# Spreading modulation sums, splitting weight sums from their copies, and other places for the last down weights, in a two-layer hybrid block

## The chip, the cores and the metric

One NeuronCore of a Trainium2 chip runs the whole program. The metric is the device time of one execution in microseconds (us), the median over the runs; lower is better. The engines are TensorE (PE, matmuls; PEld its weight loads), VectorE (DVE), ScalarE (ACT), GpSimd (POOL) and SyncE (SP). Each works through its own instructions in order. In this kernel SP and POOL do little but issue DMAs.

## The reference

A sequence of 512 tokens with 1024 features passes through two layers of three sub-blocks each. A sub-block i modulates its input, applies a function, and normalizes the gated sum:

```
mod = (silu(c) @ ada_w[layer] + ada_b[layer]).reshape(B, 3, 3, D_MODEL)
...
shift, scale, gate = mod[:, 0, None], mod[:, 1, None], mod[:, 2, None]
y = fn(x * (1 + scale) + shift)
return layer_norm(DEEPNORM_ALPHA * x + res_w * (1 + gate) * y, ln_g, ln_b)
```

The functions are, in order: SwiGLU with 2816 hidden features, `(silu(h @ w_gate) * (h @ w_up)) @ w_down`; in the first layer a mixer of a chunked mLSTM and a dilated attention, in the second one of a short convolution and a gated spatial unit; SwiGLU again. All inputs are float32.

## The kernel before

**Phases.** The program runs six phases, i = 0 to 5, one for each sub-block: feed-forward (0, 2, 3, 5), mixer 0 (1) and mixer 1 (4). Activations lie with features on partitions: X holds x, and XH and XL a high and a low part (float32r) of the modulated input. Every product of two float32 operands is made of three matmuls (`mm3`, L468 to L472): high by high, high by low, low by high. So every weight tile must be split as well: ACT copies the raw tile to its high part, DVE subtracts to get the low part (L302 and L305).

**Weights.** `plan` (L200) lists all weight tiles ("units") in their order of use. `load` (L258) issues the next raw tile's DMA on SP, with two raw buffers. `halve` (L277) takes one step of splitting the oldest raw tile: half of it, two steps to a unit. A unit's split parts go to a class of places: "w" (three places, kept through all phases) or "d" (two places of a feed-forward phase). A unit may be split when the unit so many before it in its class is done with (`ready`, L267).

**Feed-forward.** The 22 hidden tiles are worked in three chunks c of 6, 8 and 8: up (gate and up products, SiLU, product), then down, added to X by `resid` (L641), one instruction to an output tile. In chunks 1 and 2 the up part uses a Strassen-like scheme (`seven`, L766): two 4-tile halves of the contraction, two halves of the tokens, seven products instead of eight for gate and up together. It needs sums of the moving operand (`sums_of`, L740, made during the down part of chunk 0, kept in the two "d" places until the last product of chunk 2) and sums of the weights, `sr` (made in `quarter`, L313). There a unit is split in four steps, u.n = 0 to 3, and each step's parts go to one of three "w" places, used in a ring (`Ring`, L169):

- step 0: DVE makes sums 0 and 1 (L326, L327); ACT copies the raw upper tile;
- step 1: DVE makes sums 2 and 3 (L329, L330); ACT copies sums 0 and 1 (L338);
- step 2: ACT copies sums 2 and 3; step 3: ACT copies the last raw quarter.

Each step's low half (L341) is issued one piece later. `quarters` (L350) makes up for steps that are late when a product needs them.

**Order of work.** The order on every engine is written out by the program. `run` (L455) issues a list of pieces, each some 12 matmuls of 256 columns or 6 of 512, and calls `tick` (L443) after each. A tick may load; then it does one modulation sum if the count of ticks is a multiple of `ticks["ada"]`, else a step of splitting (on odd ticks, or on all where the list is "eager"), else a deferred ACT instruction. Lists called "quiet" have no ticks; there `prepare` (a load and a step) is placed by hand (SPLIT_A, SPLIT_B, SPLIT_MIX).

**Modulation.** mod is not a matmul here. For each phase there are 24 tiles of 128x1024 of ada_w: 8 of shift, 8 of scale, 8 of gate. `ada_load` (L384) brings one on POOL's queue into one of two buffers; `ada_sum` (L390) multiplies it with silu(c) and sums along the row, one DVE instruction (L392). `ada_step` does the next sum in a queue of all phases' tiles. Phase 0's first 16 are made in `start` (L1520), which interleaves them with the first weights and rows of x. Its 8 gate tiles and all of phases 1 to 5 come by ticks. ADA_EVERY (L48) gives the ticks between two sums, for the first up part of a phase, the down parts and the mixers. `ada_finish(i + 1)` in the last projection, between its first half of the tokens and its second, makes all sums of phase i + 1 that are still missing, and phase 0's missing gates are made after its first up part (L912).

**The last projection** (`last_projection`, L690) of a phase does the down products of chunk 2 for the first half of the tokens, then for the second half, with the first half's layer norm placed between the second's pieces (NORM_A): centre (L554), squares (L556, L564), statistics (L580, L512 to L526), spread (L586). The second half's norm goes between the first pieces of the next phase (NORM_B).

Of the kernel before, what the change touches and what calls it, by code (L numbers as in the profile page):

```python
# [19 lines left out]
P = 128  # L20
# [24 lines left out]
NORM_V_AT = (1, 5)  # L45


ADA_EVERY = {"up": (3, 0, 0, 0, 0, 0), "down": ((0, 2, 2), 0, (0, 2, 0), (0, 2, 0), 0, (0, 0, 0)), "mixer": (0, 4, 0, 0, 4, 0)}  # L48


C_C = 0
# [20 lines left out]
def tile_kernel(ctx, tc, prm, crow, cst, mst, oneh, relb, xin, adaw, wgu, wd6, wd8, abfm, abtm, abg, about, cdfm, cdtm, cdout,  # L72
# [127 lines left out]
    def plan():  # L200
        def add(src, shape, cls="w", i=0):
            u = Unit(src, shape, cls, i)
            units.append(u)
            members.setdefault((cls, i if cls != "w" else 0), []).append(u)

        def add_seven(src, i, ring, t):

            u = Unit(src, [2, KT, P], "s", i)
            u.ring, u.t, u.parts = ring, t, []
            units.append(u)  # L210

        def hold(i):

            held_d[i] = [Unit(None, None, "d", i) for _ in range(2)]
            members.setdefault(("d", i), []).extend(held_d[i])

        for i in range(6):
            if i in FFN_OF:
                f = FFN_OF[i]
                j0 = 0  # L220
                for c, n in enumerate(CHUNKS):
                    for j in range(j0, j0 + n):
                        if c:
                            if j == j0:
                                ring = Ring(n, i)
                                members["w", 0].extend(ring.places)
                            add_seven(wgu[f, j], i, ring, j - j0)
                        else:
                            add(wgu[f, j], [2, KT, P], "d" if j in ((3, 4) if i else (4,)) else "w", i)
                    if c == 0:  # L230
                        hold(i)
                    for g in range(4):
                        add(wd6[f, g] if n == 6 else wd8[f, c - 1, g], [2, n, P], "d" if c == 2 and g > 2 else "w", i)
                    j0 += n
            elif i == 1:
                for u in range(2):
                    add(abtm[0, u], [4, S])
                add(abfm[0], [2, KT, P])
                add(abg, [1, KT, P], "g", i)
                add(abfm[1], [2, KT, P], "k", i)  # L240
                for n in (2, 4, 3, 5):
                    add(abfm[n], [2, KT, P])
                for u in range(2):
                    add(abtm[1, u], [4, S])
                for n in (6, 7):
                    add(abfm[n], [2, KT, P])
                for c in range(2):
                    for g in range(2):
                        add(about[c, g], [4, 4, P])
            else:  # L250
                for u in range(2):
                    add(cdtm[u], [4, S])
                for n in (0, 1, 2, 3, 6, 4, 5, 7):
                    add(cdfm[n], [2, KT, P], "e" if n == 1 else "w", i)
                for g in range(4):
                    add(cdout[g], [2, KT, P], "w" if g < 3 else "e", i)
# [56 lines left out]
    def quarter(u):  # L313

        at = u.ring.part(u)
        if u.i not in sums_at or not at:
            return False
        place = u.ring.places[at[0]]
        if place.hl is None:
            if not ready(place):  # L320
                return False
            place.hl = tuple(wp.tile([P, 2, KT, P], F32R, tag="w" + x, name=nm("w" + x)) for x in "hl")
        sr = sums_at[u.i]
        a11, a12, a21, a22 = (u.raw[:, m, 4 * k:4 * k + 4, :] for m in range(2) for k in range(2))
        if u.n == 0:
            V.tensor_tensor(out=sr[:, 0], in0=a21, in1=a22, op=ALU.add)  # L326
            V.tensor_tensor(out=sr[:, 1], in0=sr[:, 0], in1=a11, op=ALU.subtract)  # L327
        elif u.n == 1:
            V.tensor_tensor(out=sr[:, 2], in0=a11, in1=a21, op=ALU.subtract)  # L329
            V.tensor_tensor(out=sr[:, 3], in0=a12, in1=sr[:, 1], op=ALU.subtract)  # L330
        src = (u.raw[:, 0], sr[:, 0:2].rearrange("p a b c -> p (a b) c"), sr[:, 2:4].rearrange("p a b c -> p (a b) c"),
               u.raw[:, 1, 4:8, :])[u.n]
        k0 = 4 * (u.t % 2) if u.n == 3 else 0
        h, l = (t[:, at[1], k0:k0 + src.shape[1], :] for t in place.hl)
        u.parts.append((h, l))
        u.n += 1
        last = u.n == 4
        A.copy(h, src)  # L338

        def low():  # L340
            V.tensor_tensor(out=l, in0=src, in1=h.bitcast(F32), op=ALU.subtract)  # L341
            u.lows += 1
            if last:
                u.split = True
                halved[0] += 1
        begun[0] += last
        after(1, low)
        return True
# [35 lines left out]
    def ada_load(i, t):  # L384
        l, s3 = divmod(i, 3)
        w = ap_.tile([P, D], F32, tag="aw", name=nm("aw"))
        nc.gpsimd.dma_start(w, adaw[l, s3 * 24 + t])  # L387
        return w

    def ada_sum(i, t, w):  # L390
# [11 lines left out]
    def ada_step():  # L402
        if not (ada_l or ada_q):
            return False
        ada_ahead()
        ada_sum(*ada_l.pop(0))
        return True
# [3 lines left out]
    def ada_scalars(i):  # L411

        g = prm_t[:, C_LNG + (i - 1) * 8:C_LNG + i * 8]
        b = prm_t[:, C_LNB + (i - 1) * 8:C_LNB + i * 8]
        At = SM([P, 8], tag="At", bufs=2)
        Bt = SM([P, 8], tag="Bt", bufs=2)
        V.scalar_tensor_tensor(out=At, in0=mod[i][:, 8:16], scalar=1.0, in1=g, op0=ALU.add, op1=ALU.mult)
        V.scalar_tensor_tensor(out=Bt, in0=mod[i][:, 8:16], scalar=1.0, in1=b, op0=ALU.add, op1=ALU.mult)
        V.tensor_tensor(out=Bt, in0=Bt, in1=mod[i][:, 0:8], op=ALU.add)
        scal["A", i], scal["B", i] = At, Bt  # L420
        ag = SM([P, 8], tag="ag", bufs=2)
        ab = SM([P, 8], tag="ab", bufs=2)
        V.tensor_scalar(out=ag, in0=g, scalar1=ALPHA, scalar2=None, op0=ALU.mult)
        V.tensor_scalar(out=ab, in0=b, scalar1=ALPHA, scalar2=None, op0=ALU.mult)
        scal["ag", i], scal["ab", i] = ag, ab

    def ada_gate(i):
        Gt = SM([P, 8], tag="Gt", bufs=2)
        V.tensor_scalar(out=Gt, in0=mod[i][:, 16:24], scalar1=1.0, scalar2=RW[i], op0=ALU.add, op1=ALU.mult)
        scal["G", i] = Gt  # L430

    def ada_finish(i):
        while ada_l and ada_l[0][0] <= i or not ada_l and ada_q and ada_q[0][0] <= i:
            ada_step()
        if i < 6:
            ada_scalars(i)
            ada_gate(i)


    defer = []  # L440
# [199 lines left out]

    def resid(i, d, ps, cs):  # L641

        V.scalar_tensor_tensor(out=X[:, d, cs], in0=ps, scalar=scal["G", i][:, d:d + 1], in1=X[:, d, cs],  # L643
                               op0=ALU.mult, op1=ALU.add)

# [87 lines left out]
    def ffn(i, f, hp):  # L733
# [119 lines left out]
        for c, n in enumerate(CHUNKS):  # L853
# [54 lines left out]
                free(u)  # L908
                jj += 1
            flush(defer)  # L910
            ticks["ada"] = ADA_EVERY["down"][i][c]
            if i == 0 and c == 0:  # L912
                while ada_l and ada_l[0][0] == 0 or ada_q and ada_q[0][0] == 0:
                    ada_step()
                ada_gate(0)

            def operands(u, d, k, cs):
                h, l = u.hl
# [6 lines left out]
                moving_sums = [f for k in range(4) for f in sums_of(k)]  # L925
            if c < len(CHUNKS) - 1:
                for g in range(4):
                    u = take()
                    ps = []
                    for d in (2 * g, 2 * g + 1):  # L930
                        if c == 0:
                            for f in moving_sums[3 * d // 2:3 * (d + 1) // 2]:
                                ps.append(lambda f=f, d=d: after(1 + (d % 2), f))
                        ps.append(pieces(lambda k, u=u, d=d: operands(u, d, k, FULL), n, S, lambda ps, d=d: resid(i, d, ps, FULL)))
                    if rest_:
                        a, b = ps
                        run([rest_[0]] + a[:2] + [rest_[1]] + b[:2] + a[2:] + b[2:], eager=True)
                        rest_ = []
                    else:
                        for p in ps:  # L940
                            if callable(p):
                                p()
                            else:
                                run(p, eager=g == 3)
                    free(u)
            else:
                us = units[used[0]:used[0] + 4]
                used[0] += 4
                last_projection(i, us, lambda d, k, cs: operands(us[d // 2], d, k, cs), n,
                                (rest_[0], lambda: (rest_[1](), free(*held_d[i]))))  # L950
# [785 lines left out]
```

## Time and profile before

| | |
|---|---|
| time, median of 3 runs | 2000.06 us (1997.52 to 2003.45) |
| the profiled execution: time | 2002.09 us |
| its span, first to last instruction | 2000.3 us |
| PE busy | 1890.6 us, 95%, 12954 matmuls |
| DVE busy | 1457.9 us, 73% |
| ACT busy | 836.9 us, 42% |
| POOL busy | 68.4 us, 3% |
| mean granted clock of PE | 0.978 |
| read from HBM | 255.41 MB |

How to read it: busy time is the time in which the engine's row of the trace shows an instruction. Matmuls are pipelined and their ends are modelled, so what tells is PE's idle time and the rate at which matmuls start. In a row of waits, "PE pa L777 <- DVE wl L341" says that a matmul of line 777 into tile pa stood still until the DVE instruction of line 341 that writes wl was through. In a row of a group of instructions, the last column is the engine's idle time before them and what ended most of it. In a row of the timeline come start, duration, engine, line, operation, out<-in, and in brackets the idle time before it. In a table of windows come the stretch (us from the start of the span), its width, each engine's busy time with the number of its instructions, the granted clock, the share of the DMA engines in use, and GB/s. PE was idle for 109.7 us of the span, in waits of up to 14 us.

### The profile page before, as it was taken

How to read it: one execution, taken by the hardware profiler on the slowest of the kernel's cores; microseconds unless marked ns; L12 is line 12 of the kernel's file. 1: busy time of each engine (PE TensorE's matmuls, PEld its weight loads, DVE VectorE, ACT ScalarE, POOL GpSimd, SP SyncE). 2: the span in 40 equal slices, each digit the busy share in tenths (PEclk: the TensorE clock that was granted, in tenths of full speed). 3: DMA queues.
4: the chain of work that ended last, by engine and by line, in shares of the span. 5: the costliest groups of instructions: out<-in, count | busy, mean ns of one | idle time of the engine just before them, and what ended most of it. 6: DMA issues, size and time to landing. Idle time of an engine off the chain costs nothing.

```text
span 2000.3 us, 31495 instructions
## 1 busy us (share of the span) xinstructions
PE 1890.6 (95%) x12954; PEld 1732.3 (87%) x12954; DVE 1457.9 (73%) x2694; ACT 836.9 (42%) x1398; POOL 68.4 (3%) x133
## 2 busy tenths in 40 slices
PE   6999989999999999998998999899699899999997
PEld 5889889888777998987998899799698799898997
DVE  6698787856566838868775588796699783884875
ACT  4445155253343544524525255153342253452541
POOL 0000100000000000010000000100001000000000
PEclk9999999999999999998999999999799999999998
DMA  9533644434453322254322224633425421232321
GB/s 344 171 106 112 211 146 142 149 131 145 136 183 93 111 70 85 105 201 148 127 96 81 89 85 142 213 120 127 137 95 211 178 93 69 84 116 85 106 106 43
DMA packets 57381, 259.56 MB, mean 130 GB/s; under 512 B 6083, under 2 KB 15724, under 8 KB 38549
## 3 DMA queue, kind: packets, MB, share of 16 engines
q1 hardware_dynamic: 38804, 190.44, 26.9%
q0 software_dynamic: 18432, 67.12, 9.9%
q8 instruction: 101, 1.65, 0.3%
q14 instruction: 44, 0.35, 0.1%
HBM read 255.41 MB, written 2.12 MB: 129 GB/s over the span
## 4 chain that ended last, share of the span: by engine, by line
issue 63%; PE 26%; DVE 4%; POOL 2%; DMA 2%; ACT 1%; SPq 0%; POOLq 0%; DVEq 0%; ACTq 0%
PE pm L470 6%; PE pm L472 6%; PE pm L471 6%; PE pm L777 4%; PE pa L777 3%; POOL aw L387 2%; DMA aw<-in_adaw 2%; DVE aw L392 1%; DVE wl L341 0%; PE pb L580 0%; ACT wh L338 0%; PE pa L543 0%; ACT w L556 0%; PE pa L1134 0%; PE pa L471 0%
## 5 line engine op out<-in xcount | busy, mean ns | idle before, releaser
L470 PE MATMUL pm<-hH,wh 128*128 128x512 f32 (+1 forms) x768 | 271.0, 353 | 11.0 <-DVE X L643 11.0
L471 PE MATMUL pm<-hL,wh 128*128 128x512 f32 (+1 forms) x768 | 269.6, 351 | 0.0
L472 PE MATMUL pm<-hH,wl 128*128 128x512 f32 (+1 forms) x768 | 269.2, 351 | 0.0
L392 DVE CUSTOM_DVE_ANT_0 aw<-aw,sc_t,prm_t 128x1024 f32<-128x1024 f32 x144 | 183.6, 1280 | 84.7 <-DMA aw<-in_adaw 84.5
L777 PE MATMUL pm<-th,wh 128*128 128x256 f32 x1024 | 239.9, 283 | 0.0
L777 PE MATMUL pa<-XH,wl 128*128 128x256 f32 x768 | 217.0, 283 | 18.5 <-DVE wl L341 18.5
L305 DVE TENSOR_TENSOR wl<-raw,wh 128x1024 fp32r<-128x1024 f32 (+1 forms) x168 | 194.8, 1169 | 51.1 <-ACT wh L302 50.8
L777 PE MATMUL pa<-XH,wh 128*128 128x256 f32 x768 | 216.2, 282 | 14.9 <-ACT pa L811 13.2
L470 PE MATMUL pm<-XH,wh 128*128 128x256 f32 (+1 forms) x632 | 214.0, 339 | 15.0 <-ACT wh L1553 14.0
L777 PE MATMUL pm<-th,wl 128*128 128x256 f32 x768 | 217.3, 283 | 0.0
L777 PE MATMUL pa<-XL,wh 128*128 128x256 f32 x768 | 215.3, 280 | 0.4 <-DVE XL L763 0.4
L471 PE MATMUL pm<-XL,wh 128*128 128x256 f32 (+1 forms) x632 | 209.6, 332 | 1.1 <-DVE XL L1601 1.1
L472 PE MATMUL pm<-XH,wl 128*128 128x256 f32 (+1 forms) x632 | 209.5, 331 | 0.0
L302 ACT CAST wh<-raw 128x1024 fp32r<-128x1024 f32 (+1 forms) x168 | 164.1, 1002 | 51.3 <-PE pm L471 26.5
L777 PEld LDWEIGHTS pm<-th,wh 128*128 128x128 f32 x1024 | 177.8, 191 | 0.4
L470 PEld LDWEIGHTS pm<-hH,wh 128*128 128x128 f32 x768 | 146.9, 191 | 31.6 <-DVE X L643 11.2
L341 DVE TENSOR_TENSOR wl<-sr,wh 128x1024 fp32r<-128x1024 f32 x128 | 156.3, 1221 | 15.9 <-ACT wh L338 14.5
L338 ACT CAST wh<-sr 128x1024 fp32r<-128x1024 f32 x128 | 134.0, 1047 | 80.7 <-DVE sr L327 49.3
L472 PEld LDWEIGHTS pm<-hH,wl 128*128 128x128 f32 x768 | 146.5, 191 | 20.5
L471 PEld LDWEIGHTS pm<-hL,wh 128*128 128x128 f32 x768 | 146.8, 191 | 20.0
L777 PEld LDWEIGHTS pa<-XH,wl 128*128 128x128 f32 x768 | 146.6, 191 | 19.6 <-DVE wl L341 19.5
L643 DVE SCALAR_TENSOR_TENSOR X<-pm,sm,X 128x256 f32<-128x256 f32 (+1 forms) x168 | 97.4, 582 | 87.8 <-PE pm L472 87.8
(295 smaller groups left out, 4557.8 us busy)
## 6 DMA issues: line engine op xcount, KB each, us to landing
raw<-in_wgu SPq DMA_DIRECT2D x84, 1024.0 KB, 4.8
aw<-in_adaw POOLq DMA_DIRECT2D x128, 512.0 KB, 3.9
raw<-in_wd SPq DMA_DIRECT2D x32, 1024.0 KB, 4.8
raw<-in_wd SPq DMA_DIRECT2D x16, 768.0 KB, 4.3
aw<-in_adaw SPq DMA_DIRECT2D x16, 512.0 KB, 8.6
raw<-in_abfm SPq DMA_DIRECT2D x8, 1024.0 KB, 4.8
raw<-in_cdfm SPq DMA_DIRECT2D x8, 1024.0 KB, 6.2
raw<-in_wgu SPq DMA_DIRECT2D x16, 256.0 KB, 8.6
```

What stands on the lines that cost most here:

```text
L302: A.copy(u.hl[0][:, x], u.raw[:, x])
L305: V.tensor_tensor(out=u.hl[1][:, x], in0=u.raw[:, x], in1=u.hl[0][:, x].bitcast(F32), op=ALU.subtract)
L338: A.copy(h, src)
L341: V.tensor_tensor(out=l, in0=src, in1=h.bitcast(F32), op=ALU.subtract)
L387: nc.gpsimd.dma_start(w, adaw[l, s3 * 24 + t])
L392: V.tensor_tensor_reduce(out=w, in0=w, in1=sc_t, scale=1.0, scalar=prm_t[:, c0:c0 + 1], op0=ALU.mult, op1=ALU.add, accum_out=mod[i][:, t:t ...
L470: T.matmul(ps, st[0], mv[0], start=first, stop=False)
L471: T.matmul(ps, st[0], mv[1], start=False, stop=False)
L472: T.matmul(ps, st[1], mv[0], start=False, stop=last)
L643: V.scalar_tensor_tensor(out=X[:, d, cs], in0=ps, scalar=scal["G", i][:, d:d + 1], in1=X[:, d, cs], op0=ALU.mult, op1=ALU.add)
L777: T.matmul(ps_, s_, v_, start=first and k + x == 0, stop=k == 3 and x == 2, skip_group_check=not first)
```

## The change

- The counts of ADA_EVERY change. A down part's count no longer depends on the phase: none in chunks 0 and 2, every third tick in chunk 1. The first up parts of phases 2, 3 and 5 get sums too (every third tick); that of phase 0 every second tick, the mixers every third. Phase 0's last down part keeps every second tick.
- In the last quarter (g == 3) of a down part of chunks 0 and 1 no sums are made.
- `ada_finish` makes only the first 16 tiles (shift and scale) of the next phase. The gates may come later, at the latest before the first `resid` of their phase. The list of phase 0's missing gates after its first up part goes.
- Phase 0's tiles that come by ticks (the 8 gates) are loaded on SP's queue, in the program's order, not on POOL's.
- In `quarter` sums 2 and 3 are a step of their own, between steps 0 and 1; a unit takes five steps.
- Of the four groups of down weights of chunk 2 the last two are of class "d", not the last alone, so they take the places that held the moving sums.

```diff
-ADA_EVERY = {"up": (3, 0, 0, 0, 0, 0), "down": ((0, 2, 2), 0, (0, 2, 0), (0, 2, 0), 0, (0, 0, 0)), "mixer": (0, 4, 0, 0, 4, 0)}
+ADA_EVERY = {"up": (2, 0, 3, 3, 0, 3), "down": (0, 3, 0), "mixer": (0, 3, 0, 0, 3, 0)}
...
-                        add(wd6[f, g] if n == 6 else wd8[f, c - 1, g], [2, n, P], "d" if c == 2 and g > 2 else "w", i)
+                        add(wd6[f, g] if n == 6 else wd8[f, c - 1, g], [2, n, P], "d" if c == 2 and g > 1 else "w", i)
...
-        elif u.n == 1:
+        elif not u.summed:
             V.tensor_tensor(out=sr[:, 2], in0=a11, in1=a21, op=ALU.subtract)
             V.tensor_tensor(out=sr[:, 3], in0=a12, in1=sr[:, 1], op=ALU.subtract)
+            u.summed = True
+            return True
...
-        nc.gpsimd.dma_start(w, adaw[l, s3 * 24 + t])
+        (nc.gpsimd if i else nc.sync).dma_start(w, adaw[l, s3 * 24 + t])
...
+    def ada_until(i, n):
+        while (ada_l or ada_q) and (ada_l or ada_q)[0][:2] < (i, n):
+            ada_step()
+
     def ada_finish(i):
-        while ada_l and ada_l[0][0] <= i or not ada_l and ada_q and ada_q[0][0] <= i:
-            ada_step()
         if i < 6:
+            ada_until(i, 16)
             ada_scalars(i)
-            ada_gate(i)
...
     def resid(i, d, ps, cs):
 
+        if ("G", i) not in scal:
+            ada_until(i, 24)
+            ada_gate(i)
...
-            ticks["ada"] = ADA_EVERY["down"][i][c]
-            if i == 0 and c == 0:
-                while ada_l and ada_l[0][0] == 0 or ada_q and ada_q[0][0] == 0:
-                    ada_step()
-                ada_gate(0)
+            ticks["ada"] = 2 if i == 0 and c == 2 else ADA_EVERY["down"][c]
...
             if c < len(CHUNKS) - 1:
                 for g in range(4):
+                    if g == 3:
+                        ticks["ada"] = 0
```

More of the change, by code (lines that the diff above doesn't have):

```diff
@@ L208, in add_seven @@
             u = Unit(src, [2, KT, P], "s", i)
-            u.ring, u.t, u.parts = ring, t, []
+            u.ring, u.t, u.parts, u.summed = ring, t, [], False
             units.append(u)
```

## The prediction

> **What bounds the kernel now.** I read the page first, then what TensorE (PE) waited for, then stretches of the span around each wait, then the order of the work inside three of them. All times are those of the profiled execution: 2002.09 us, of which 2000.3 are its span; the median of the runs is 2000.06, so I subtract from the one and give the answer on the other.
>
> ```profile
> span 2000.3 us, 31495 instructions
> PE 1890.6 (95%) x12954; PEld 1732.3 (87%) x12954; DVE 1457.9 (73%) x2694; ACT 836.9 (42%) x1398; POOL 68.4 (3%) x133
> L392 DVE CUSTOM_DVE_ANT_0 aw<-aw,sc_t,prm_t 128x1024 f32<-128x1024 f32 x144 | 183.6, 1280 | 84.7 <-DMA aw<-in_adaw 84.5
> ```
>
> PE is the bound: 95% busy, 110 us idle. No matmul is removed, so the change can only win idle time, and time in which the matmuls run slowly. The third row is the suspect: 144 modulation sums of 1.28 us on VectorE (DVE), before which DVE sat 84.5 us waiting for their tiles. DVE works in order, so whatever is queued behind such a sum waits too. Who among PE's work paid for it?
>
> ```profile
> PE pa L777 <- DVE wl L341: 18.5, 5, 6.2
> PE pb L580 <- DVE w L564: 14.9, 5, 7.9
> PE pm L470 <- ACT wh L1553: 14.0, 1, 14.0
> PE pa L777 <- ACT pa L811: 13.2, 8, 1.8
> PE pm L470 <- DVE X L643: 13.0, 4, 11.0
> PE pa L543 <- DVE w L651: 4.3, 1, 4.3
> PE pm L471 <- DVE wl L305: 3.1, 1, 3.1
> PE pm L470 <- ACT dh L302: 2.9, 2, 1.9
> PE pm L472 <- DVE dl L305: 2.3, 3, 0.8
> ```
>
> (Columns: us in total, times, longest.) Waits of 3 to 14 us carry most of it, nearly all on DVE: low halves of weights (L341, L305), norm and residual (L564, L643, L651). Their places, one row for each:
>
> ```profile
> core 0: us, PE busy (x) PEld busy (x) DVE busy (x) ACT busy (x) POOL busy (x), PEclk, DMA share, GB/s
> 118.00:126.00 8.00, 4.89 (x32) 4.07 (x31) 7.62 (x15) 2.27 (x5) 0.00 (x0) 1.00 0.00 1
> 255.00:268.00 13.00, 7.83 (x46) 7.33 (x45) 11.50 (x16) 5.06 (x9) 1.05 (x2) 0.74 0.57 205
> 902.00:920.00 18.00, 10.98 (x79) 10.28 (x77) 15.43 (x25) 5.21 (x10) 2.65 (x5) 0.81 0.66 220
> 1015.00:1034.00 19.00, 15.13 (x111) 14.82 (x110) 14.11 (x41) 3.35 (x5) 1.59 (x3) 0.91 0.26 84
> 1060.00:1082.00 22.00, 16.76 (x122) 15.74 (x121) 15.14 (x28) 11.66 (x21) 0.00 (x0) 0.92 0.34 123
> 1290.00:1302.00 12.00, 5.38 (x31) 4.98 (x31) 10.06 (x15) 3.50 (x6) 1.06 (x2) 0.72 0.59 203
> 1395.00:1428.00 33.00, 20.23 (x142) 19.63 (x141) 21.30 (x52) 4.30 (x6) 3.72 (x7) 0.79 0.34 112
> 1440.00:1453.00 13.00, 9.88 (x35) 7.73 (x35) 9.22 (x17) 6.76 (x9) 0.00 (x0) 0.74 0.62 208
> 1585.00:1609.00 24.00, 16.09 (x104) 15.65 (x103) 16.79 (x45) 4.65 (x7) 1.06 (x2) 0.79 0.21 65
> 1850.00:1863.00 13.00, 12.46 (x99) 11.89 (x98) 8.53 (x12) 6.71 (x12) 0.00 (x0) 1.00 0.22 81
> ```
>
> Width less PE's busy time is its idle time. The last row is the control: the third chunk of the last feed-forward layer (phase 5) starts with no sums before it and idles 0.5 us; the three like starts behind a down projection full of sums (255, 902, 1290) idle 5.2, 7.0 and 6.6. Eight rows also show a granted clock (PEclk) well under 1.
>
> **The sums, counted.** A tick follows each piece of matmul work (12 matmuls of 256 columns or 6 of 512, 1.4 us); ADA_EVERY says how many ticks lie between two sums. Counting ticks (16 in phase 0's first chunk, 34 in a middle down projection, of which the last 8 now take none, 18 in a last projection, 106 in mixer 0, 28 in a later first chunk, 80 in mixer 1), I get for the new kernel: phase 0 does its 8 gate sums in the 16 ticks, then 9 and 9; mixer 0 does 36 where it did 26; phases 2 and 3 do 9 and 10 in their first chunks and 9 and 8 in the middle; mixer 1 does 27 where it did 20; phase 5 the last 3. At the end of each phase the next one needs only its first 16 tiles: it has 18, 24, 24, 18 and 21. So no burst is left in ada_finish, where the old count left 3, 7 and 4 sums (1015, 1395, 1585), nor after the first chunk (3).
>
> *Bursts at a phase's end.* Idle 3.9, 12.8 and 7.9 us. What is late next is the norm's own chain, centre, squares, statistics, which these rows put behind the sums; I leave 2 us in all. Gain 22.6 (bounds 15 to 24).
>
> *Starts of the third chunk.* 17.5 us gained against the control (18.8 less three times 0.5), since the last quarter of the down projection now splits weights on every tick and the sums before it come every third tick (4.2 us) instead of every second, at which DVE waited for tiles (84.5 us in all). Bounds 10 to 17.5.
>
> *Phase 0, first chunk.* The 3.1 us at 118 follow from the burst of three that held the moving sums back; 2.6 gained (0 to 3.1).
>
> *Start.* PE begins at 14.0, with DMA saturated. Two tiles that are not needed for 50 us go first on POOL's queue:
>
> ```profile
> 1.26 1.19 POOL L387 DMA_DIRECT2D aw<-in_adaw  x2 [0.81 <-POOLq L1724]
> 0.00:20.00 20.00, 6.03 (x14) 4.64 (x15) 9.28 (x18) 7.03 (x10) 1.39 (x6) 1.00 0.92 327
> aw<-in_adaw POOLq DMA_DIRECT2D x128, 512.0 KB, 3.9
> ```
>
> On SP they queue behind the start's loads: 1 MB at 327 GB/s is 3.2 us less in the way. I take 2 (0 to 3.2). In exchange SP now waits for a sum before each of the six later tiles, with the raw weight loads for the first down projection behind it, and those feed the split on ACT and DVE; a sum every second tick is 2.8 us against 3.9 to land, two in flight: cost 1 (0 to 3).
>
> *The place.* The third group of last down weights waited for ring place 2, and that place is left with the last product, exactly when the moving sums' places are; so the group itself is no earlier or later. But place 2 is then free for the next phase's first unit, which formerly waited for a group to finish its second half. Its two steps (copy and low half) move into the first half's idle ticks, and every later step of SPLIT_A reaches one unit further. That takes away most of the weight waits at 1060 (5.2 us: dh 2.9, dl 2.3) and 1440 (3.1): gain 7.8 (4 to 8.3).
>
> *Slow tails.* After each of these idles the granted clock is halved for a while:
>
> ```profile
> 261.00:266.00 5.00, 4.53 (x21) 4.24 (x21) 4.96 (x8) 3.07 (x6) 0.00 (x0) 0.50 0.80 285
> 934.00:938.00 4.00, 4.00 (x22) 4.00 (x23) 3.98 (x6) 2.75 (x4) 0.00 (x0) 0.62 0.67 250
> 1603.00:1607.00 4.00, 4.00 (x21) 4.00 (x21) 3.28 (x14) 0.00 (x0) 0.00 (x0) 0.50 0.00 0
> 1880.00:1900.00 20.00, 20.00 (x174) 20.00 (x173) 18.45 (x29) 11.60 (x20) 0.00 (x0) 1.00 0.30 106
> ```
>
> At full clock 174 matmuls take 20 us, 0.115 each; 21 took 4 us at 1603, so 1.6 us was lost there, and about 2 at 261. Eight idles that I remove or shorten have such a tail: 8 x 1.6 = 12.8 us (6 to 16). [...]
>
> *Sums one step ahead.* A unit of the seven products now takes five steps, not four; same instructions. In that stretch DVE is 18.45 of 20 us busy, so their order matters. Here is the second unit's first sum copy, and what bounds it:
>
> ```profile
> 1851.99 1.38 PE pm L777 x12
> ```
>
> ```profile
> 1858.51 1.05 ACT L338 CAST wh<-sr 128x1024 fp32r<-128x1024 f32 x1 [0.30 <-DVE sr L327]
> 1861.07 1.22 DVE L341 TENSOR_TENSOR wl<-sr,wh 128x1024 fp32r<-128x1024 f32 x1
> 1861.18 0.42 ACT L822 ACTIVATE w<-w 128x256 f32<-128x256 f32 x1 [1.62 <-DVE w L821]
> 1875.04 0.36 ACT L811 COPY pa<-pm 128x256 f32<-128x256 f32 x1
> 1884.42 0.37 ACT L811 COPY pa<-pm 128x256 f32<-128x256 f32 x1
> ```
>
> The chunk starts at 1852.0. One tick later the copy falls behind L822: L822 ends at 1861.6, the copy 1.05 later, its low half 1.22 after that, at 1863.9. PE wants it after seven products of 1.4, the 0.5 idle and two matmuls, at 1862.6: a new wait of 1.3. In return a copy of half the length stands before the L811 of 1875.04, where the fourth unit's first one stood; L811 comes some 0.5 earlier and PE 1.3 later, so its wait of 1.8 goes. The L811 after it (1884.42) has 0.5 to spare now; DVE has lost 0.8 by waiting for the late copy, and PE, 1.8 less 1.3 the earlier, comes 0.5 sooner: 0.8 late. Sum 1.3 + 0.8 - 1.8 = 0.3 in each of eight chunks; I take 2 us in all, bounds -8 and +9 (1 us each way per chunk).
>
> *Where the sums go.*
>
> ```profile
> 697.00:737.00 40.00, 40.00 (x311) 38.42 (x310) 11.43 (x19) 16.28 (x28) 0.00 (x0) 1.00 0.23 80
> 1466.00:1549.00 83.00, 83.00 (x432) 70.14 (x431) 78.64 (x237) 28.05 (x39) 6.91 (x13) 1.00 0.42 154
> 440.00:650.00 210.00, 209.29 (x1252) 168.40 (x1251) 133.40 (x325) 80.14 (x167) 12.22 (x23) 1.00 0.43 143
> ```
>
> Each sum brings its 512 KB load on POOL along; it lands in 3.9 us, under three ticks, so DVE should not wait for it. In the first chunks DVE has 28 us free in 40 and nine sums need 11.5: nothing (a sum takes a tick from a split there; the splits have ticks to spare). In mixer 0 ten more sums, 12.8 us, fall into 77 us of idle DVE, but among dependent steps: cost 2 (0 to 5). In mixer 1 DVE is idle 4.4 us of 83; 14 sums there become about 19, 6.4 us more; PE runs up to three result buffers ahead, which hides part: cost 4 (0 to 8).
>
> Phase 0's last projection keeps a sum every second tick, and so its 4.3 us (L651).
>
> **Sum.** 22.6 + 17.5 + 2.6 + 2 + 7.8 + 12.8 = 65.3 gained; 1 + 2 + 2 + 4 = 9 lost; net 56.3. From 2002.09 that is 1945.8; on the median of 2000.06, **1944**.
>
> **Rivals.**
>
> *The waits move.* The sums' cost returns where they now sit: mixer 1 pays its 8, mixer 0 its 5, the seven products their 9, SP its 3, and the bounds of the gains are all low (15 + 10 + 0 + 0 + 4 + 6 = 35). Net 10: 1990. Between that and the forecast, half way, 1967. For: mixer 1's 78.64 of 83. Against: the first chunks' 28 free us. Chance 0.14 for 1960 to 1990.
>
> [...] Chance 0.12. [...]
>
> *DVE becomes the bound of the seven products; slower.* DVE's 18.45 of 20 us leaves 0.75 us free in a unit of seven products (7 x 12 x 0.115 = 9.7 us). If the later copy adds more than that to DVE's waiting in each of the 64 units, PE waits in all of them; from 0.75 + 56.3/64 = 1.6 us on the kernel is slower, at 2.0 by 24 us: 2024. Against: in the steady part only the copy of the first two sums moves, by a tick, with seven ticks to its product. Chance 0.05.
>
> *The freed place does nothing*, because the raw tile has not landed or the place is not the limit: 7.8 and two tails (3.2) less, 1955. Chance 0.1.
>
> **How the numbers follow.** The forecast has 0.59. The range: low, the forecast with the seven products at their better bound (10 less) and the mixers free (6): 1928; high 1970, through the middle of the moved waits. A measurement of this kernel tells 0.3%, 6 us. Faster 0.92; same 0.03, the end of the moved waits; slower 0.05.
>
> **What would show it.** In the new profile: no row of L392 with three sums in a row at a phase's end; idle near 0.5 us at every third chunk's start; the waits on X L643 (11.0) and w L564 (7.9) at 1 or less; PE's first matmul near 12; the L811 waits of 1.8 gone and a wait on L341 near 1 in their place; DVE over 95% in mixer 1, PE idle there 2 to 4. PE idle near 66 in all. The prediction is wrong if a wait on DVE of several us stands in a mixer, or in every unit of the seven products.

## The result, and the profile after

The changed kernel takes 1936.05 us (median of 4 runs, 1935.02 to 1944.65) against 2000.65 of the kernel before on the same chip (4 runs): a ratio of 0.9687 (95% interval 0.9656 to 0.9718). The forecast was 1944, between 1928 and 1970. By the medians 64.6 us are gained, some 8 more than forecast. The profiled execution is the slowest of the four, 1944.65 us; against the 2002.09 on which the sum was made that is 57.4 less, where the sum said 56.3. Line numbers shift: L341, L392, L580, L643, L777, L811 of before are L343, L394, L584, L650, L784, L818 now.

The page of the kernel after, then its groups by line:

```profile
span 1942.9 us, 31456 instructions
...
PE 1878.5 (97%) x12954; PEld 1718.1 (88%) x12954; DVE 1455.0 (75%) x2694; ACT 833.9 (43%) x1398; POOL 64.2 (3%) x125
```

```profile
L394 DVE CUSTOM_DVE_ANT_0 aw<-aw,sc_t,prm_t 128x1024 f32<-128x1024 f32 x144 | 183.4, 1279 | 42.8 <-DMA aw<-in_adaw 42.8
```

DVE does the same 144 sums in the same time. What fell is its wait for their tiles, 84.7 to 42.8 us, and with it PE's idle time: 109.7 to 64.4. PE's busy time fell too, by 12.1, with the same 12954 matmuls: their mean granted clock rose from 0.978 to 0.991. What PE waits for now (us in total, times, longest):

```profile
PE pm L474 <- ACT wh L1558: 11.8, 1, 11.8
PE pa L784 <- DVE wl L343: 6.1, 8, 0.8
PE pa L784 <- ACT pa L818: 5.6, 8, 0.8
PE pa L547 <- DVE w L658: 5.3, 1, 5.3
PE pm L784 <- DVE wl L343: 4.3, 8, 0.5
PE pb L584 <- DVE w L568: 4.2, 3, 2.9
PE pm L474 <- ACT t L150: 2.9, 1, 2.9
PE pm L474 <- DVE X L650: 1.6, 2, 1.1
PE pm L474 <- ACT hH L150: 1.5, 1, 1.5
```

Behind the start itself nothing is left over 5.3 us. The 11.0 on X and the 7.9 on w are gone. The third row's longest is 0.8, where the wait on L811 was 1.8; the second row is the new wait of the seven products, 0.76 in each of eight chunks. The places, in the order of the terms of the sum (stretch, width, PE busy, and so on):

```profile
core 0: us, PE busy (x) PEld busy (x) DVE busy (x) ACT busy (x) POOL busy (x), PEclk, DMA share, GB/s
110.00:126.00 16.00, 16.00 (x99) 14.17 (x98) 15.20 (x29) 7.06 (x14) 0.00 (x0) 1.00 0.04 8
248.00:262.00 14.00, 12.62 (x103) 12.01 (x102) 11.93 (x17) 7.89 (x15) 0.00 (x0) 1.00 0.31 101
900.00:914.00 14.00, 12.63 (x104) 12.02 (x103) 11.86 (x19) 7.81 (x13) 0.00 (x0) 1.00 0.42 151
1256.00:1270.00 14.00, 12.62 (x103) 12.01 (x103) 11.89 (x17) 7.89 (x15) 0.00 (x0) 1.00 0.32 101
1796.00:1810.00 14.00, 12.62 (x104) 12.01 (x103) 12.34 (x18) 8.00 (x15) 0.00 (x0) 1.00 0.35 113
1003.00:1014.00 11.00, 10.53 (x89) 10.32 (x88) 9.74 (x29) 4.72 (x8) 0.00 (x0) 1.00 0.00 0
1362.00:1383.00 21.00, 21.00 (x179) 21.00 (x178) 18.70 (x48) 10.83 (x19) 0.00 (x0) 1.00 0.01 2
1565.00:1590.00 25.00, 24.42 (x208) 24.24 (x208) 20.81 (x48) 17.53 (x29) 0.00 (x0) 1.00 0.37 126
1052.00:1070.00 18.00, 18.00 (x160) 18.00 (x160) 9.33 (x16) 8.33 (x15) 1.59 (x3) 1.00 0.33 111
1383.00:1403.00 20.00, 17.14 (x83) 13.99 (x82) 14.48 (x35) 9.27 (x14) 0.00 (x0) 0.91 0.47 157
1403.00:1525.00 122.00, 116.59 (x643) 100.09 (x642) 108.72 (x287) 41.08 (x59) 12.22 (x23) 0.99 0.53 190
420.00:640.00 220.00, 218.36 (x1291) 175.74 (x1290) 140.73 (x325) 87.38 (x176) 16.47 (x31) 0.99 0.47 158
```

The four third-chunk starts (248, 900, 1256, 1796) are now alike to 0.01 us: three that idled 5.2 to 7.0 have become the control. The three phase ends (1003, 1362, 1565) idle 0.5, 0 and 0.6 us where the bursts cost 3.9, 12.8 and 7.9. Two rows are not clean. At 1383 PE idles 2.9 us and the clock falls: phase 4's beginning, where before stood the 3.1 us of the row at 1440. And mixer 1 (1403) has 5.4; in the like stretch of before PE was busy for all of 122 us:

```profile
1456.00:1578.00 122.00, 122.00 (x707) 106.64 (x706) 108.58 (x287) 43.10 (x63) 10.02 (x19) 1.00 0.49 181
```

### The profile page after: what moved, and what is told of

It is laid out like the page before. It is cut to its first block, busy times and chain, and to the rows that moved or that the text cites. A ratio compares the mean times of both kernels' runs of the same rounds, so it can differ in the third digit from the quotient of the medians.

```text
span 1942.9 us, 31456 instructions
## 1 busy us (share of the span) xinstructions
PE 1878.5 (97%) x12954; PEld 1718.1 (88%) x12954; DVE 1455.0 (75%) x2694; ACT 833.9 (43%) x1398; POOL 64.2 (3%) x125
## 4 chain that ended last, share of the span: by engine, by line
PE 66%; DVE 14%; issue 12%; DMA 4%; ACT 3%; POOL 1%; SPq 0%; DVEq 0%; POOLq 0%; ACTq 0%
PE pm L474 14%; PE pm L475 14%; PE pm L476 14%; PE pm L784 11%; PE pa L784 8%; DVE wl L343 3%; DMA aw<-in_adaw 2%; DMA raw<-in_wgu 1%; ACT wh L340 1%; PE pa L1270 1%; DVE wl L305 1%; DVE aw L394 1%; DVE sr L327 1%; DVE sr L329 1%; PE pm L1294 1%
## 5 line engine op out<-in xcount | busy, mean ns | idle before, releaser
L784 PE MATMUL pm<-th,wh 128*128 128x256 f32 x1024 | 238.5, 281 | 0.0
L474 PE MATMUL pm<-hH,wh 128*128 128x512 f32 (+1 forms) x640 | 234.1, 366 | 1.5 <-ACT hH L150 1.5
L475 PE MATMUL pm<-hL,wh 128*128 128x512 f32 (+1 forms) x640 | 231.3, 361 | 0.2 <-DVE hL L153 0.2
L476 PE MATMUL pm<-hH,wl 128*128 128x512 f32 (+1 forms) x640 | 231.4, 361 | 0.0
L474 PE MATMUL pm<-XH,wh 128*128 128x256 f32 (+1 forms) x632 | 215.1, 340 | 13.7 <-ACT wh L1558 11.8
L784 PE MATMUL pa<-XH,wh 128*128 128x256 f32 x768 | 215.4, 281 | 6.2 <-ACT pa L818 5.6
L784 PE MATMUL pa<-XH,wl 128*128 128x256 f32 x768 | 214.7, 280 | 6.1 <-DVE wl L343 6.1
L784 PE MATMUL pm<-th,wl 128*128 128x256 f32 x768 | 216.0, 281 | 0.0
L305 DVE TENSOR_TENSOR wl<-raw,wh 128x1024 fp32r<-128x1024 f32 (+1 forms) x160 | 185.3, 1167 | 40.8 <-ACT wh L302 40.3
L394 DVE CUSTOM_DVE_ANT_0 aw<-aw,sc_t,prm_t 128x1024 f32<-128x1024 f32 x144 | 183.4, 1279 | 42.8 <-DMA aw<-in_adaw 42.8
L784 PE MATMUL pa<-XL,wh 128*128 128x256 f32 x768 | 213.6, 278 | 0.0
L650 DVE SCALAR_TENSOR_TENSOR X<-pm,sm,X 128x256 f32<-128x256 f32 (+1 forms) x168 | 97.7, 582 | 121.5 <-PE pm L476 120.8
L302 ACT CAST wh<-raw 128x1024 fp32r<-128x1024 f32 (+1 forms) x160 | 156.2, 1000 | 51.7 <-PE pm L475 12.6
L784 PEld LDWEIGHTS pm<-th,wh 128*128 128x128 f32 x1024 | 175.9, 189 | 0.4
L343 DVE TENSOR_TENSOR wl<-sr,wh 128x1024 fp32r<-128x1024 f32 x128 | 156.3, 1221 | 25.3 <-ACT wh L340 24.0
L784 PEld LDWEIGHTS pa<-XH,wh 128*128 128x128 f32 x768 | 145.2, 189 | 9.5 <-ACT pa L818 7.2
L784 PEld LDWEIGHTS pa<-XH,wl 128*128 128x128 f32 x768 | 144.2, 188 | 7.7 <-DVE wl L343 7.7
L474 PEld LDWEIGHTS pm<-XH,wh 128*128 128x128 f32 x632 | 120.1, 190 | 28.5 <-ACT wh L1558 11.8
L784 PEld LDWEIGHTS pm<-th,wl 128*128 128x128 f32 x768 | 145.1, 189 | 0.0
## 6 DMA issues: line engine op xcount, KB each, us to landing
raw<-in_wgu SPq DMA_DIRECT2D x16, 256.0 KB, 8.4
```

The costliest lines, as they stand in the source:

```text
L302: A.copy(u.hl[0][:, x], u.raw[:, x])
L305: V.tensor_tensor(out=u.hl[1][:, x], in0=u.raw[:, x], in1=u.hl[0][:, x].bitcast(F32), op=ALU.subtract)
L394: V.tensor_tensor_reduce(out=w, in0=w, in1=sc_t, scale=1.0, scalar=prm_t[:, c0:c0 + 1], op0=ALU.mult, op1=ALU.add, accum_out=mod[i][:, t:t ...
L474: T.matmul(ps, st[0], mv[0], start=first, stop=False)
L475: T.matmul(ps, st[0], mv[1], start=False, stop=False)
L476: T.matmul(ps, st[1], mv[0], start=False, stop=last)
```

## The experiments

Theory: PE pays for DVE work that is queued ahead of the few instructions that gate it, at the phase ends and the third-chunk starts, so what counts is where the sums stand; the other parts are worth a few us each. Rivals: the freed place does nothing; the seven products' order matters, either way; the waits merely move into the mixers. Four kernels each take one part of the change back, two split the spreading, three carry it further, one repeats. A difference below is that of the ratios times 2003 us, against the repeat's 0.9689; the intervals are some 0.0018 to each side, so a difference is known to 5 us.

**The change again.** Edit: none.

> The changed kernel once more, as the measure for the three beside it. The profiled execution took 1944.65 us and the three others 1935.0 to 1936.8. If the first stands alone: 1935 to 1937. If executions of this kernel differ by 8 us among themselves: a spread of several us here too, and then parts under 4 us can't be told apart.

1939.89 us (1938.10 to 1944.02), ratio 0.9689 (0.9671 to 0.9708). One kernel's executions lie up to 10 us apart (the 1935.02 and 1944.65 above), so terms of 1 to 3 us can be read in a trace but not in a time.

**One last group in the "d" places, as before.**

```diff
-"d" if c == 2 and g > 1 else "w"
+"d" if c == 2 and g > 2 else "w"
```

> The change without its places: the third group of last down weights is of class w again. Theory (the place stood in the way of the next phase's first unit): waits on low and high halves of weights come back at the starts of phases 3 and 4, 7.8 us of idle and two slow tails of 1.6, so 9 to 11 us slower than the changed kernel. Rival (those waits came from the bursts of sums before them, which are gone anyway): 0 to 3 us slower.

0.9740 (0.9722 to 0.9758), 10 us slower than the change. PE's waits:

```profile
PE pm L475 <- DVE wl L305: 3.2, 1, 3.2
PE pm L474 <- ACT dh L302: 2.8, 2, 1.9
PE pm L476 <- DVE dl L305: 2.3, 3, 0.8
```

These are the rows of before (3.1, 2.9, 2.3), 8.3 us together, and no other large wait of before came back; in exchange the change's wait of 2.9 on L568 is gone. The place works. PE is idle 69.8 us, against 64.3 in the change's profile and 60.6 in the repeat's, so 5.5 to 9.2 of the 10 us are idle time.

**Sums 2 and 3 in one step with the copy, as before.**

```diff
-        elif not u.summed:
+        elif u.n == 1:
...
-            u.summed = True
-            return True
```

> The change with sums 2 and 3 of the weights made in the same step as the copy of sums 0 and 1. Theory (the order of the copies matters little: per chunk idles of 0.5 + 0.8 + 0.8 now, 0.5 + 1.8 then): 0 to 1 us per chunk apart, so the eight chunks 0 to 3 us slower, and up to 5 more where the wait of 1.8 on the copy of L811's kind is followed by half clock (in the kernel before 2 of 8). Rival (the late copy costs in every unit): faster by 5 or more.

0.9682 (0.9662 to 0.9701): no difference. Yet the waits trade places (line numbers are two lower here):

```profile
PE pa L782 <- ACT pa L816: 13.5, 8, 1.8
```

The 1.8 us in every chunk are back, and the row of 6.1 us on the low halves is gone. Two things of about one size exchanged; the five-step order is worth nothing that a time can show here.

**Phase 0's gate tiles on POOL's queue.**

```diff
-        (nc.gpsimd if i else nc.sync).dma_start(w, adaw[l, s3 * 24 + t])
+        nc.gpsimd.dma_start(w, adaw[l, s3 * 24 + t])
```

> The change with phase 0's gate tiles on POOL's queue again. Theory: the first matmul comes 2.2 us later again (14.0 against 11.8), and the wait of 1.5 us at 88 on ACT's copy of the hidden tile goes, if SP's waiting made it: 0 to 2.5 us slower. Rival (the gain of the start is taken back in phase 0 in any case): no difference.

0.9721 (0.9705 to 0.9738), 6 us slower: more than expected. PE's waits, then DVE's timeline:

```profile
PE pm L474 <- ACT wh L1558: 14.0, 1, 14.0
PE pm L474 <- ACT hH L150: 4.5, 1, 4.5
```

```profile
90.80 1.28 DVE L394 CUSTOM_DVE_ANT_0 aw<-aw,sc_t,prm_t 128x1024 f32<-128x1024 f32 x1 [4.45 <-DMA aw<-in_adaw]
```

The start loses 2.2 us (14.0 against 11.8), as priced. The rest is at 90: with the sums at every second tick DVE stands 4.45 us for a tile, and the product of a hidden tile (L875), which ACT rounds to hH, is queued behind that sum. POOL asked for the tile at 82.33, SP for raw weights at 82.93, and the tile landed 8.3 us after its issue. On SP the two kinds of loads follow one another (at 79.99 and 82.89 in the change), and the wait on hH is 1.5. The queue of its own brought the tile no sooner (its sum starts at 90.80, in the change, on SP, at 85.84), and gave up the order. That the raw weights held the tile up is what these times suggest; no run shows it by itself.

**The old counts** (old ADA_EVERY, bursts at the phase ends and after phase 0's first chunk, no pause in the last quarter), with all other parts of the change.

```diff
+ADA_EVERY = {"up": (3, 0, 0, 0, 0, 0), "down": ((0, 2, 2), 0, (0, 2, 0), (0, 2, 0), 0, (0, 0, 0)), "mixer": (0, 4, 0, 0, 4, 0)}
...
-            ada_until(i, 16)
+            ada_until(i, 24)
...
-                    if g == 3:
-                        ticks["ada"] = 0
```

> The other three parts without the spreading: the old counts of ticks, sums also in the last quarter of a down part, all 24 tiles before the next phase's norm. Theory (the spreading is the greatest part and the parts add up): the bursts' 22.6, the third chunks' 17.5, the first chunk's 2.6 and their tails of some 9 come back, and the mixers' 4 to 6 go: 44 to 48 us slower than the changed kernel, about 1986. Rival (the freed place or the step of its own already took part of those waits away): 25 to 35 slower.

0.9941 (0.9926 to 0.9957), 50 us slower. PE's waits:

```profile
PE pa L784 <- DVE wl L343: 22.6, 14, 4.6
PE pb L584 <- DVE w L568: 17.3, 6, 7.6
PE pm L474 <- DVE X L650: 13.0, 4, 11.0
```

The three waits are the first, second and fifth of before, 18.5, 14.9 and 13.0. The spreading is most of the change; the four parts taken back one by one sum to 50 + 10 + 6 - 1 = 65 us against 62 for all together. With each difference known to 5 us, no action of one part on another shows.

**The middle down part at every second tick, last quarter included.**

```diff
-            ticks["ada"] = 2 if i == 0 and c == 2 else ADA_EVERY["down"][c]
+            ticks["ada"] = 2 if i == 0 and c == 2 or i < 5 and c == 1 else ADA_EVERY["down"][c]
...
-                    if g == 3:
-                        ticks["ada"] = 0
```

> The change with a sum every second tick in the middle down parts of phases 0, 2 and 3, the last quarter too, so 17 sums there instead of 9. Theory (sums before the third chunk make its start late): its starts in those phases idle 5 to 7 us again, 17.5 in all with tails of 1 to 1.7 each, about 21; mixer 1 is left with 5 sums and gains 4 to 6: 15 to 18 us slower. Rival (only the lateness of the old splits made it, not the sums in the last quarter): under 5 slower.

0.9777 (0.9758 to 0.9796), 18 us slower. DVE's timeline ahead of phase 0's third chunk:

```profile
253.54 1.28 DVE L394 CUSTOM_DVE_ANT_0 aw<-aw,sc_t,prm_t 128x1024 f32<-128x1024 f32 x1 [1.14 <-DMA aw<-in_adaw]
...
254.75 1.22 DVE L343 TENSOR_TENSOR wl<-sr,wh 128x1024 fp32r<-128x1024 f32 x1
```

A low half that PE needs stands right behind a sum that had itself waited 1.14 us for its tile; PE idled 3.4 us there until 256.0. The three starts together (245 to 268, 896 to 916, 1265 to 1292) idle 18.9 us, against 4.1 in the change. In return mixer 1, with fewer sums left for it, idles 1.4 instead of 5.4. So the 18 us are the third-chunk term with its tails, less what mixer 1 gained. The edit raises the rate and drops the pause at once; where phase 0 has the higher rate with the pause ("And two waits more", below), its start idles only 2.0 more than in the change, so at that start the lost pause is the larger part.

**All 24 tiles by the phase's end.**

```diff
-            ada_until(i, 16)
+            ada_until(i, 24)
```

> The kernel after, but ada_finish makes all 24 tiles of the next phase again, gates too, not only the first 16. By the count of ticks phase 0 ends with 18 of phase 1's tiles made, so a burst of six sums stands there; later the counts run ahead (30 in mixer 0 and so on), so the other phase ends have bursts of none to two. Theory (a burst at a phase's end costs PE nearly its whole DVE time, since the norm chain queues behind it): six sums are 7.7 us if their tiles wait in the buffers, some 15 us if each waits for its load; the burst of seven before idled PE 12.8 us, so 8 to 11 us slower here, tail of slow matmuls included. Rival (with the spread counts the last projection has slack enough to swallow six sums): 0 to 3 us slower.

0.9779 (0.9762 to 0.9796), 18 us slower: the theory's side, but 8 to 11 was too little. PE's wait, then DVE's timeline:

```profile
PE pb L584 <- DVE w L568: 21.1, 4, 16.9
```

```profile
361.67 1.28 DVE L394 CUSTOM_DVE_ANT_0 aw<-aw,sc_t,prm_t 128x1024 f32<-128x1024 f32 x1 [1.59 <-DMA aw<-in_adaw]
...
375.02 1.28 DVE L394 CUSTOM_DVE_ANT_0 aw<-aw,sc_t,prm_t 128x1024 f32<-128x1024 f32 x1 [1.39 <-DMA aw<-in_adaw]
```

Six sums start from 361.67 to 375.02, one in 2.7 us: 1.28 of work and the rest waiting, since a tile's load is issued only when one of two buffers is free again. Six cost 16 us of DVE, and PE idled 16.9 in one piece. In the kernel before the seven sums took as long for each (1397.3 to 1415.5), but PE worked on for 8.3 us, then waited for the first residual behind them, 1.0 us on, and idled 11.0 (and 1.8 later). Here PE worked on for only 4.6 us, and what it waits for, the squares of the norm, ends 5.3 us behind the last sum: 16.2 + 5.3 - 4.6 = 16.9. The estimate carried the idle time over; a burst costs its period times its sums, plus the work queued behind it that PE needs, less PE's work in hand at that place.

**Mixer 1 at every fourth tick, the first parts of phases 2 and 3 at every second.**

```diff
+ADA_EVERY = {"up": (2, 0, 2, 2, 0, 3), "down": (0, 3, 0), "mixer": (0, 3, 0, 0, 4, 0)}
```

> The change with a sum every second tick in the first chunks of phases 2 and 3, where VectorE is idle for half of the time or more, and every fourth tick in mixer 1, as before. Theory (VectorE is nearly full in mixer 1 and the seven sums more there cost PE 2 to 4 us, waits on ACT's t and on the low halves there, with a tail): 2 to 5 us faster than the changed kernel. Rival (those waits are the mixer's own): no difference.

0.9649 (0.9629 to 0.9669), 8 us faster than the change; its interval and the repeat's just fail to meet. In mixer 1 PE no longer idles:

```profile
1403.00:1525.00 122.00, 122.00 (x695) 106.15 (x695) 107.88 (x286) 43.09 (x63) 9.56 (x18) 0.99 0.49 180
```

The change idles 5.4 us there, its repeat 3.5 (116.54 busy of 120). So the extra sums in mixer 1 did cost about what was feared; whether the rest of the 8 us is real, times known to 5 us can't tell.

**And two waits more,** on top of the run before. Phase 0's middle down part at every second tick and its last one at every fourth; the multiplication of the mask of mixer 1's spatial weights (L1415, DVE) behind the first pieces of the mixer.

```diff
-            ticks["ada"] = 2 if i == 0 and c == 2 else ADA_EVERY["down"][c]
+            ticks["ada"] = (0, 2, 4)[c] if i == 0 else ADA_EVERY["down"][c]
...
-        V.tensor_tensor(out=wsT, in0=wsT, in1=TRI.unsqueeze(1).to_broadcast([P, 4, P]), op=ALU.mult)
...
         run(ps, ex, True)
+        V.tensor_tensor(out=wsT, in0=wsT, in1=TRI.unsqueeze(1).to_broadcast([P, 4, P]), op=ALU.mult)
```

> The same with two more edits. In phase 0 the middle down part takes a sum every second tick up to its last quarter, and the last projection every fourth: the wait of 4.3 to 6.5 us on L658's sum (5.3 in the changed kernel) and its tail should shrink to 1 or 2. And mixer 1's multiplication of the mask into wsT, which stands at the head of VectorE's work for phase 4 and waits 4.2 us for its DMA while the norm's chain stands behind it, moves behind the first list of pieces: the wait of 2.9 us on the squares at the end of phase 3 goes, with a tail of 1.7. Theory: 6 to 9 us faster than mix4. Rival (the norm's chain is then next and as late): 0 to 3.

1923.16 us (1922.02 to 1923.22), ratio 0.9593 (0.9578 to 0.9608): 19 us under the change and 11 under the run before, where 6 to 9 were expected: the fastest of all. PE's waits:

```profile
PE pa L784 <- DVE wl L343: 8.0, 9, 2.0
...
PE pb L584 <- DVE w L568: 2.3, 3, 1.0
```

The 5.3 on L658 and the 2.9 on L568 are gone. A new one of 2.0 on L343, at 247.6, is the price of every second tick in phase 0's middle.

**The same, with phase 0 at every third tick in both parts.**

```diff
-            ticks["ada"] = (0, 2, 4)[c] if i == 0 else ADA_EVERY["down"][c]
+            ticks["ada"] = 3 if i == 0 and c == 2 else ADA_EVERY["down"][c]
```

> The fastest kernel so far (mixer 1 every fourth tick, first parts of phases 2 and 3 every second, the mask multiply moved), but phase 0's middle down projection at every third tick and its last projection at every third, so that nine and six sums come and one is left to ada_finish. Theory (a sum every second tick in the middle down makes DVE wait for tiles: 2.0 us of PE wait at the start of the third chunk): that wait goes, and the one sum left costs 1.3 us of DVE ahead of the norm, 1 to 4 us if its tile must still land: -2 to +3 us beside the fastest. Rival (a third-chunk start waits for the last quarter's splits whatever the sums do): the 2.0 stays, and it is 1 to 4 us slower.

0.9625 (0.9611 to 0.9639), 6 us slower than the fastest; neither side had it whole. The 2.0 went, as the theory said and the rival denied, but the sum that is left for the phase's end costs more than 4. DVE's timeline there, then PE's wait:

```profile
355.76 1.28 DVE L394 CUSTOM_DVE_ANT_0 aw<-aw,sc_t,prm_t 128x1024 f32<-128x1024 f32 x1 [3.65 <-DMA aw<-in_adaw]
```

```profile
PE pb L584 <- DVE w L568: 6.1, 3, 4.8
```

DVE waits 3.65 for the tile, then sums, and the norm is 4.8 late. That is 1.8 us net of the 2.0 won and the 1.0 there before. PE's idle time grew by only 1.4 us in all (54.7 to 56.2), its busy time by 7.5 (1866.7 to 1874.2) with the same matmuls: the mean granted clock is 0.993 against 0.996, and from 735 to 739 it was 0.60. By these two clocks some 6 of the 7.5 are slow matmuls (0.003 x 1930), an estimate that their rounding leaves open by 2 us.

## Why the prediction was right

The time and the total were right because the large terms were read at their places. By the profiles, in us (gain positive; "slow tails" is the fall of PE's busy time, 1890.6 to 1878.5, with the same matmuls):

| term | forecast | measured |
|---|---|---|
| bursts at phase ends | 22.6 | 24.6 - 1.1 = 23.5 |
| starts of the third chunk | 17.5 | 18.8 - 4.1 = 14.7; with the new product wait of 3 x 0.76 put to the steps, 17.0 |
| first chunk | 2.6 | 3.1 |
| start | 2 | 14.0 - 11.8 = 2.2 |
| freed place | 7.8 | 5.2 + 0.3 = 5.5 |
| slow tails | 12.8 | 12.1 |
| SP's queue | -1 | -1.5 (the wait on hH; below, whose it is) |
| seven products | -2 | 13.2 - 5.6 - 6.1 + 3.6 - 4.3 = +0.8 |
| mixer 0 | -2 | 0.7 - 1.6 = -0.9 |
| mixer 1 | -4 | -5.4 |
| sum | 56.3 | 56.4, of 57.4 |

That the sum comes this close is partly luck. Single terms miss by up to 2.8 us, in both directions, and the misses cancel. And the 57.4 belong to the slowest execution of the change: its repeat, profiled at 1938.24 us, idles 60.6 and is busy 1875.8, 6.4 us less. One term was also added wrongly: 18.8 less three times 0.5 is 17.3, not 17.5.

**Right by its reasons.** Bursts and starts: the old counts alone give back 50 us, with the same waits. The freed place: the row at 1052 is full, and taking the place back returns the three waits at 1050 and 1395; the rival that it does nothing is out. The seven products: the new wait came where the working put it, on the low half of the second unit's first sums, 0.76 rather than 1.3, and the 1.8 on L811 went. The rival that DVE becomes the bound there needed 1.6 us in each of 64 units; there are eight waits of 0.8. The rival that the waits merely move into the mixers holds for 6.3 us of them (0.9 and 5.4), not for the whole.

**Wrong in part.** The step "that takes away most of the weight waits at 1060 and 1440" held at 1060 only. At 1440 the low half of L305 was late because DVE stood 4.0 us at the mask multiplication for its tile, with the low half queued next. With the freed place the low half is no longer behind it; the norm is, and PE waits 2.9 (DVE's timeline of the kernel before, then after):

```profile
1442.59 0.69 DVE L1410 TENSOR_TENSOR wsT<-wsT,cst_t 128x512 f32<-128x512 f32 x1 [4.02 <-DMA wsT<-in_sguw]
1443.20 2.35 DVE L305 TENSOR_TENSOR wl<-raw,wh 128x1024 fp32r<-128x1024 f32 x2
```

```profile
1388.87 0.69 DVE L1415 TENSOR_TENSOR wsT<-wsT,cst_t 128x512 f32<-128x512 f32 x1 [4.24 <-DMA wsT<-in_sguw]
...
1391.87 0.68 DVE L568 TENSOR_TENSOR w<-w,w 128x512 f32<-128x512 f32 x1
```

So the sign that "w L564" would be at 1 or less failed, and the cause was a wait of DVE itself, on a DMA, that the prediction had left out.

"DVE over 95% in mixer 1" was wrong: 108.72 of 122 us, 89%, no more than before (108.58). It is place again that costs: 2.9 of PE's 5.4 us came where a sum sat ahead of the gated product (L1490) that ACT rounds for PE (t, L150); from 1499.8 to 1514 DVE was busy for 12.01 of 14.2 us:

```profile
1511.35 1.28 DVE L394 CUSTOM_DVE_ANT_0 aw<-aw,sc_t,prm_t 128x1024 f32<-128x1024 f32 x1
...
1512.56 0.68 DVE L1490 TENSOR_TENSOR w<-w,pm 128x512 f32<-128x512 f32 x1
```

The repeat has no wait on t but 2.3 on L305; with fewer sums neither is there. That DVE would not wait for tiles at every third tick was too much as well: 4.9 us of its 42.8 are in mixer 1.

"SP's queue, cost 1" had the wrong sign. It was argued from loads that follow in order; what it left out is that the tiles can come later still without that order. With them on POOL the wait is 4.5, on SP 1.5. The 1.5 itself comes from a sum at every second tick: with the old counts, on SP as well, there is no wait on hH.

**The tails** were right in size, partly by luck, but not as 1.6 us for each idle; that is the next section but one.

## What to carry to other kernels

A long in-order queue is paid for at the few places where the other engine runs dry, so spread filler work away from them; the same 184 us of sums cost some 50 us more or less by their places alone. Price a burst by its period, with the reload of its buffers in it (2.7 us here), not by its busy time (1.28). And when a wait is credited to the change, look at what its releaser itself stood behind: the wait at phase 4's beginning only changed hands.

## What the runs showed of the hardware

The granted clock fell and rose on a fixed grid in the two traces laid out here. In the clock records of the kernel before all 15 half-clock stretches begin whole multiples of 3.413 us apart, to 0.02 us (the first at 126.00, the last at 1986.27: 545 x 3.4133), and all but the last, which lasts to the end of the work, are 3.41, 6.83 or 10.24 us long. The six of the kernel after lie likewise (357.74 to 1927.87: 460 x 3.4133). Windows of the kernel before, cut at that grid:

```profile
core 0: us, PE busy (x) PEld busy (x) DVE busy (x) ACT busy (x) POOL busy (x), PEclk, DMA share, GB/s
143.07:146.48 3.41, 2.88 (x25) 2.69 (x23) 2.72 (x6) 1.55 (x4) 0.00 (x0) 1.00 0.02 5
146.48:149.89 3.41, 2.14 (x18) 2.14 (x19) 3.38 (x6) 2.92 (x6) 0.00 (x0) 1.00 0.60 214
...
931.55:934.96 3.41, 1.61 (x14) 1.41 (x13) 3.38 (x6) 2.46 (x5) 0.00 (x0) 1.00 0.33 72
934.96:938.37 3.41, 3.41 (x18) 3.41 (x17) 3.38 (x6) 2.08 (x4) 0.00 (x0) 0.50 0.56 235
...
1873.63:1877.04 3.41, 1.62 (x14) 1.58 (x14) 3.38 (x6) 2.87 (x5) 0.00 (x0) 1.00 0.49 144
1877.04:1880.46 3.42, 3.42 (x31) 3.42 (x30) 3.38 (x5) 1.78 (x4) 0.00 (x0) 1.00 0.42 170
```

The wait on L811 is 1.8 us in each of these three places. At 932 it falls within one window, PE is busy for less than half of it, and the next window runs at half clock, with 18 matmuls instead of 31; the like wait at 795 does the same. At 146 the same wait is split over two windows, and nothing happens, nor at 1180 and 1747, where it is split too. At 1873 it lies within one window, right at its beginning, and the clock stays.

Laid on their grids, the two traces show where the bound lies (from 24 to 1900 us, full-clock windows): all 13 in which PE was busy for less than 1.5 us were followed by half clock, 3 of 6 with 1.5 to 1.9 us, and above that 3 of some 1050. These 3 lie between 453 and 679 us, in mixer 0 and just behind it (at 675.55 of the kernel before and 668.35 of the kernel after PE was busy for 2.4 us); in the third, at 453.31 of the kernel after, PE was busy throughout, mostly with small matmuls, moving 4x4 to 64x128. No run here shows what halves the clock there. The grid's first line lies 3.12 us behind the span's start in the trace of before, 2.75 in that of after.

So 1.8 us idle within a window of 3.41 was enough in two places of three. That short idles have no tail, which had a chance of 0.12, is out, but so is a fixed 1.6 for each: what a short wait cost here depended on where it fell on the grid. The forecast of 12.8 came near 12.1 partly by luck: the stretches that went were one to three windows long, PE stood idle in part of them (7.3 of the 10.24 us from 1409.41), and two new ones came (at 457 and 1515 of the kernel after).

That the executions of one kernel lie up to 10 us apart would fit a grid that lies at another place in each of them, but no run here tested it.
